# mLSTM trunk on one core: causal mask applied in the copy of the scores, three convolution steps given to the odd chunk

## The chip, the cores and the metric

The kernel runs on one core of a Trainium2 chip. The metric is the time of one execution in device microseconds; the number compared is the median of several runs. The engines are named as in the profile: PE is TensorE's matmul stream (PEld its weight loads), DVE is VectorE, ACT is ScalarE, POOL is GpSimd, and SP is the queue that issues most DMAs.

## The reference

One layer of a hybrid decoder on x (1, 4096, 1024): RMSNorm, one input projection, a pooling branch, an mLSTM branch with 4 heads of 256, an output projection, a residual sum and a final RMSNorm. What the change touches is the chunkwise mLSTM with chunks of 128 rows, inside which every row sees only itself and earlier rows:

```
xc = silu(causal_conv(mx, conv_w, conv_b))          # 4 taps
q, k = headwise(xc, w_q), headwise(xc, w_k)
v = headwise(mx, w_v)
...
mask = tril(ones(CHUNK, CHUNK))
d_log = where(mask, b[:, None] - b[None, :] + ig[None, :], -inf)
W = exp(d_log - m_t[..., None]) * einsum('bhcld,bhcsd->bhcls', q, k)
num = einsum('bhcls,bhcse->bhcle', W, v) + inter * (C_s q)
```

## The kernel before, in words

The program has three stages. The first (to about 800 us) normalises x and computes the pooling branch. The second (about 800 to 1740 us) projects the mLSTM input, convolves it and runs the 32 chunks. The third computes the output gates, the second gate path and the output projection with a Strassen-like scheme. Products in fp32 are made of three fp32r matmuls, high times high, high times low and low times high, so almost every operand exists as a pair of tiles. `split` (L103) makes the pair: ACT copies the high part (L104), and DVE, or POOL where that is asked for, subtracts it from the raw value to get the low part (L105).

In the second stage three generators advance side by side for chunk n.

- `front(n)` has 13 steps, each called an "f". Steps 1 to 3 make v (L774, the copies in L776). Steps 4 and 5 make the q side, `qg` (L784, copied by ACT in L786); step 5 needs channels 4 to 7 of the convolved input `xc`. Steps 6 and 7 make the scores (L795): ACT copies 128x256 of them out of PSUM into `sc` (L797), and DVE copies the gate sums into `part` (L798). Steps 8 and 9 turn `xc` (L804). Step 10 makes the forget gates `lf` (L808 to L815) and PE turns them (L818). Steps 11 and 12 run the two scans and spread the result over the partitions (L824 to L851). Step 13 makes the decay `dm`: ACT writes four exponentials (L863), POOL sets the entries of future rows to zero (L864), DVE multiplies by the scores (L866), and `split` (L867) makes the pair `wt`, which sits in the pool named `st`. Step 13 also makes the pairs `qi` (L872 on DVE, L874 on ACT, L875 on POOL).
- `back(n-1)` has 13 steps, each a "b". For each head it computes the numerator `num` (L901 from `wt` and v, L905 from `qi` and the state), then updates the state (L930 on PE, L931 on DVE). The third matmul of L901 needs the low part of `wt`, the last thing that step 13 makes.
- `project` of the next block of 256 rows has 17 steps, the first of them before the chunk pair and the others each a "p". The mLSTM input of two channel groups of 128 is projected in four steps (L111 to L113 into `acc`), then copied out by ACT (L750) and given its last tap (L755).

After every fourth "p" a `tail` waits in a list: six multiply-adds of DVE (L673) in two steps of three, and a third step, SiLU: three activations of ACT (L695 to L697), a product of DVE (L698) and a store (L699). A "c" in the order advances the first tail of the list by one step. There are four tails in a pair of chunks, called t0 to t3 here; the channels 6 and 7 of t3 are needed by step 5 of the next even chunk.

`ORDER` (L31) writes out the order of f, b, p and c, one string for even chunks and one for odd ones. Behind the string the kernel finishes step 13 of `front`, and after an odd chunk also the projection and the tails (L978 to L988). This order of the code is a priority: the framework's planner lays out each engine's queue by its own model of time and takes, whenever an engine comes free, the first in order among those that are ready by that model. Each engine then works its queue strictly in that planned order.

Of the kernel before, what the change touches and what calls it, by code (L numbers as in the profile page):

```python
# [8 lines left out]
F32 = mybir.dt.float32  # L9
# [3 lines left out]
ALU = mybir.AluOpType  # L13
# [4 lines left out]
P = 128  # L18
# [5 lines left out]
H = 4  # L24
# [3 lines left out]
TB = 256  # L28


ORDER = ("ffffbbffbpbffbpffppccbbbcbfpbfbbpppccc", "ffffbbbfpfffpbfbfppbccbbccfpbfpbppbbcc")  # L31
VA = P + 1
GW = P + 8

# [20 lines left out]
def tile_hybrid(  # L55
# [16 lines left out]
    nc = tc.nc  # L72
# [30 lines left out]
    def split(raw, hi, lo, eng=None):  # L103
        nc.scalar.copy(out=hi, in_=raw)  # L104
        (eng or nc.vector).tensor_tensor(out=lo, in0=raw, in1=hi.bitcast(F32), op=ALU.subtract)  # L105
# [274 lines left out]
    with tc.tile_pool(name="a_st", bufs=4) as stp, \  # L380
# [147 lines left out]
        for b in range(NB):  # L528
# [6 lines left out]
            for j in range(NJ):  # L535
                g = j // 2
                win = WINDOWS[g]
                ps = accp.tile([P, T], F32, name="acc")
# [12 lines left out]
                while step < win:  # L551
# [3 lines left out]
                                            op=ALU.add)  # L555
                    cur, lo_c, step = nxt, a, step * 2
                dlt = cur[:, HALO:]
                if b == 0:
# [4 lines left out]
                                               op0=ALU.mult, op1=ALU.subtract)  # L563
# [22 lines left out]
    with tc.tile_pool(name="b_mx", bufs=NJ) as mxp, \  # L586
# [35 lines left out]
        parts = [one.tile([64 + H, P], BF16, name=f"parts{i}") for i in range(2)]  # L622
        for t in parts:
            nc.vector.memset(t, 0.0)
        bif = one.tile([P, 8], F32, name="bif")
        nc.sync.dma_start(out=bif, in_=b_if.partition_broadcast(P))

# [12 lines left out]
        for j in range(NJ):  # L640
            bqT, bkT, bvT = ({j: t[j // 4][:, j % 4]} for t in bqkv)
            ps = mapp.tile([P, T], F32, name="map")
# [121 lines left out]
        def front(n, c, mx, xc):  # L764
# [6 lines left out]
            for w, (j0, nj) in enumerate(((0, 3), (3, 3), (6, 2))):  # L771
                ps = mapp.tile([P, 3, GW], F32, name="map")
# [8 lines left out]
            for q in range(2):  # L781
                ps = mapp.tile([P, 4, P], F32, name="map")
# [6 lines left out]
            sc = wk.tile([P, H, P], F32, name="sc", bufs=1)  # L789
            for q in range(2):  # L790
                ps = mapp.tile([P, 2, GW], F32, name="map")
                for hh in range(2):
                    for t in range(2):
                        j = 4 * q + 2 * hh + t
                        nc.tensor.matmul(ps[:, hh, :], lhsT=xc[j][:, l0:l0 + P], rhs=qg[:, j, :],  # L795
                                         start=t == 0, stop=t == 1)
                nc.scalar.copy(out=sc[:, 2 * q:2 * q + 2, :], in_=ps[:, :, 0:P])  # L797
                nc.vector.tensor_copy(out=part[:, :, 3 + 2 * q:5 + 2 * q], in_=ps[:, :, P:].rearrange("p i g -> p g i"))  # L798
                yield
            for q in range(2):  # L800
                if xs is not None:
                    ps = mapp.tile([P, 4, P], F32, name="map")
                    for i in range(4):
# [25 lines left out]
                                         op0=ALU.add, op1=ALU.add)  # L829
# [31 lines left out]
            dm = wk.tile([P, H, P], F32, name="dm", bufs=1)  # L861
            for h in range(H):
                nc.scalar.activation(out=dm[:, h, :], in_=dp[:, h, :], func=AF.Exp, bias=ibc[:, h:h + 1])  # L863
            nc.gpsimd.affine_select(out=dm, in_=dm, compare_op=ALU.is_ge, fill=0.0, base=0,  # L864
                                    pattern=[[0, H], [1, P]], channel_multiplier=-1)
            nc.vector.tensor_tensor(out=dm, in0=sc, in1=dm, op=ALU.mult)  # L866
            split(dm, wt[:, 0], wt[:, 1])  # L867
            qi = []
            for h in range(H if n else 0):
                q = wk.tile([P, 2, 2, P], F32R, name="qi", bufs=4)  # L870
                raw = wk.tile([P, 2, P], F32, name="qr", bufs=4)
                nc.vector.tensor_tensor(out=raw, in0=qg[:, 2 * h:2 * h + 2, 0:P],  # L872
                                        in1=inter[:, h:h + 1, :].broadcast_to([P, 2, P]), op=ALU.mult)
# [95 lines left out]
        for n in range(NB * NCH + 1):  # L969
            fr = Steps(front(n, n % 2, *xin), 13) if n < NB * NCH else None  # L970
            turn = {"f": fr, "b": bk, "p": proj}
            for what in ORDER[n % 2]:
                if what == "c":
                    step_tail()
                elif turn[what] is not None:
                    turn[what].step()
            if bk is not None:
                bk.finish()  # L978
            if fr is None:
                break  # L980
            if n + 1 == NB * NCH:
                proj.finish()
            bk = Steps(back(n // NCH, n % NCH, *fr.finish()), 5 if n + 1 == NB * NCH else 13)
            bk.step()
            if n % 2 and n + 2 < NB * NCH:
                xin = proj.finish()
                finish_tails()
                proj = start((n + 3) // 2) if (n + 3) // 2 < NS else Steps(next_operands(), 11)  # L988
# [311 lines left out]
```

## Time and profile before

| | us |
|---|---|
| median of 3 runs (3122.46 to 3127.13) | 3122.95 |
| the profiled execution | 3121.92 |
| its span, first to last instruction | 3120.2 |
| PE busy in the span | 2916.4 (93%) |
| DVE busy | 2103.1 (67%) |
| ACT busy | 1371.2 (44%) |
| POOL busy | 897.8 (29%) |

The profile lists each engine's busy time and idle time, and puts an idle stretch down to the instruction that ended it. The timeline gives start, duration, engine, line, output and input, and in brackets the idle time before and its releaser. In the answer for stretches of time the columns are the stretch, its length, busy time of each engine with its instructions, the granted TensorE clock as a share of the full one, the DMA share and GB/s. An instruction of DVE or ACT that follows another without waiting may start before the end of that other one as the profile writes it.

### The profile page before, as it was taken

The page shows a single profiled execution, that of the slowest core. Times are in us where ns is not written, and L with a number is a line of the kernel's source. Part 1 is how long each engine was busy: PE and PEld are TensorE (multiplying, and loading weights), DVE is VectorE, ACT ScalarE, POOL GpSimd, SP SyncE. Part 2 cuts the span into 40 slices and gives each one's busy share as a digit, 9 for nine tenths or more (in the row PEclk, how much of TensorE's full clock was granted, in tenths as well). Part 3 has the DMA queues.
Part 4 walks back from the last instruction along what each step waited for, and adds up shares of the span by engine and source line. Part 5 has one row for each costly group of instructions (what it writes and reads, how often), then busy time and mean ns, then how long its engine had stood idle before and what let it go on. Part 6 is the DMA issues. An engine that isn't in the chain of part 4 may idle for free. (4 is left out here: it accounts for less than half of the span.)

```text
span 3120.2 us, 44964 instructions
## 1 busy us (share of the span) xinstructions
PE 2916.4 (93%) x15912; PEld 2527.6 (81%) x15912; DVE 2103.1 (67%) x4107; ACT 1371.2 (44%) x2722; POOL 897.8 (29%) x955
## 2 busy tenths in 40 slices
PE   7999999998989999999998897998989899989998
PEld 6888888887889989989987676887777788867887
DVE  6555555564678878878878643667667866676666
ACT  4222222211667676677677311235556633343332
POOL 1122333333255455455453222001111133320000
PEclk9999999998999999999999899999999999999999
DMA  6344455545221121121123588686677888886664
GB/s 213 115 159 154 157 185 187 184 156 189 85 65 48 49 67 49 49 68 49 48 74 93 212 277 288 222 273 209 228 244 235 273 268 277 276 293 206 211 209 170
DMA packets 258001, 531.59 MB, mean 170 GB/s; under 512 B 28528, under 2 KB 72048, under 8 KB 257776
## 3 DMA queue, kind: packets, MB, share of 16 engines
q1 hardware_dynamic: 225952, 412.84, 38.4%
q10 hardware_dynamic: 31824, 115.88, 12.1%
q8 instruction: 125, 2.05, 0.3%
q14 instruction: 100, 0.82, 0.1%
HBM read 331.49 MB, written 197.13 MB: 169 GB/s over the span
## 5 line engine op out<-in xcount | busy, mean ns | idle before, releaser
L111 PE MATMUL ps<-w,sr 128*128 128x512 f32 x1320 | 524.1, 397 | 28.0 <-ACT sr L104 19.6
L113 PE MATMUL ps<-w,sr 128*128 128x512 f32 x1320 | 520.4, 395 | 15.1 <-DVE sr L105 15.0
L112 PE MATMUL ps<-w,sr 128*128 128x512 f32 x1320 | 521.3, 395 | 0.0
L105 DVE TENSOR_TENSOR sr<-sr 128x1024 fp32r<-128x1024 f32 x221 | 285.6, 1295 | 299.8 <-ACT sr L104 298.8
L104 ACT CAST sr<-sr 128x1024 fp32r<-128x1024 f32 x221 | 231.1, 1048 | 529.2 <-PE ps L112 274.3
L111 PE MATMUL acc<-u,w 128*128 128x512 f32 x1024 | 398.8, 390 | 1.5 <-ACT u L104 1.5
L112 PE MATMUL acc<-u,w 128*128 128x512 f32 x1024 | 398.8, 389 | 0.0
L113 PE MATMUL acc<-u,w 128*128 128x512 f32 x1024 | 398.6, 389 | 0.0
L111 PEld LDWEIGHTS ps<-w,sr 128*128 128x128 f32 x1320 | 252.5, 191 | 84.4 <-ACT sr L104 21.7
L113 PEld LDWEIGHTS ps<-w,sr 128*128 128x128 f32 x1320 | 251.5, 191 | 71.6 <-DVE sr L105 19.1
L111 PE MATMUL acc<-xu,w 128*128 128x256 f32 x992 | 295.7, 298 | 0.0
L112 PEld LDWEIGHTS ps<-w,sr 128*128 128x128 f32 x1320 | 252.2, 191 | 52.8 <-issue 0.7
L113 PE MATMUL acc<-xu,w 128*128 128x256 f32 x992 | 287.2, 290 | 0.0
L112 PE MATMUL acc<-xu,w 128*128 128x256 f32 x992 | 284.4, 287 | 0.0
L661 POOL TENSOR_TENSOR cs<-c,cs 128x516 fp32r<-128x516 f32 x124 | 177.7, 1433 | 219.9 <-ACT cs L660 193.5
L673 DVE SCALAR_TENSOR_TENSOR xc<-mx,col,xc 128x256 f32<-128x256 f32 x384 | 221.6, 633 | 13.1 <-ACT xc L755 11.5
L111 PEld LDWEIGHTS acc<-u,w 128*128 128x128 f32 x1024 | 192.1, 188 | 42.3 <-ACT u L104 2.2
L113 PEld LDWEIGHTS acc<-u,w 128*128 128x128 f32 x1024 | 192.2, 188 | 40.2
L112 PEld LDWEIGHTS acc<-u,w 128*128 128x128 f32 x1024 | 192.2, 188 | 40.1
L111 PEld LDWEIGHTS acc<-xu,w 128*128 128x128 f32 x992 | 194.0, 196 | 1.2
L112 PEld LDWEIGHTS acc<-xu,w 128*128 128x128 f32 x992 | 194.1, 196 | 0.1
L113 PEld LDWEIGHTS acc<-xu,w 128*128 128x128 f32 x992 | 193.8, 195 | 0.0
(229 smaller groups left out, 5968.1 us busy)
## 6 DMA issues: line engine op xcount, KB each, us to landing
sr<-us_d ACTq DMA_DIRECT2D x112, 512.0 KB, 5.2
us_d<-st SPq DMA_DIRECT2D x64, 512.0 KB, 2.7
sr<-ym_d ACTq DMA_DIRECT2D x56, 512.0 KB, 4.4
sr<-yp_d ACTq DMA_DIRECT2D x53, 512.0 KB, 5.5
st<-in_x_t_dram SPq DMA_DIRECT2D x32, 512.0 KB, 6.0
yp_d<-sg SPq DMA_DIRECT2D x64, 256.0 KB, 2.7
st<-us_d SPq DMA_DIRECT2D x32, 512.0 KB, 5.8
xu<-us_d SPq DMA_DIRECT2D x64, 256.0 KB, 3.6
```

The costliest lines, as they stand in the source:

```text
L104: nc.scalar.copy(out=hi, in_=raw)
L105: (eng or nc.vector).tensor_tensor(out=lo, in0=raw, in1=hi.bitcast(F32), op=ALU.subtract)
L111: nc.tensor.matmul(ps, lhsT=a[0], rhs=b[0], start=start and k == 0, stop=False, skip_group_check=skip)
L112: nc.tensor.matmul(ps, lhsT=a[0], rhs=b[1], start=False, stop=False, skip_group_check=skip)
L113: nc.tensor.matmul(ps, lhsT=a[1], rhs=b[0], start=False, stop=stop and k == n - 1, skip_group_check=skip)
L661: nc.gpsimd.tensor_tensor(out=t[:, 1], in0=cst[h], in1=t[:, 0].bitcast(F32), op=ALU.subtract)
L673: nc.vector.scalar_tensor_tensor(out=a[:, t], in0=m[:, t, i:i + TB], scalar=conv_w[:, jj * 4 + i:jj * 4 + i + 1], in1=a[:, t], op0=ALU.mul ...
```

## The change

The zeroing on POOL goes. Instead a 128x128 tile `causal` of ones and zeros is made once, and the copy of the scores out of PSUM becomes a DVE product with that tile, in steps 6 and 7 of `front`, in place of ACT's copy. As the decay of future rows is now not zeroed and may overflow, the product of decay and scores first limits the decay to 3e38. In the order, the "ccc" at the end of the even chunk (all of tail t1) moves into the odd chunk, behind its first "p".

```
-ORDER = ("ffffbbffbpbffbpffppccbbbcbfpbfbbpppccc", "ffffbbbfpfffpbfbfppbccbbccfpbfpbppbbcc")
+ORDER = ("ffffbbffbpbffbpffppccbbbcbfpbfbbppp", "ffffbbbfpcccfffpbfbfppbccbbccfpbfpbppbbcc")
...
+        causal = one.tile([P, P], F32, name="causal")
+        nc.vector.memset(causal, 1.0)
+        nc.gpsimd.affine_select(out=causal, in_=causal, compare_op=ALU.is_ge, fill=0.0, base=0,
+                                pattern=[[1, P]], channel_multiplier=-1)
...
-                nc.scalar.copy(out=sc[:, 2 * q:2 * q + 2, :], in_=ps[:, :, 0:P])
+                nc.vector.tensor_tensor(out=sc[:, 2 * q:2 * q + 2, :], in0=ps[:, :, 0:P],
+                                        in1=causal.unsqueeze(1).broadcast_to([P, 2, P]), op=ALU.mult)
...
-            nc.gpsimd.affine_select(out=dm, in_=dm, compare_op=ALU.is_ge, fill=0.0, base=0,
-                                    pattern=[[0, H], [1, P]], channel_multiplier=-1)
-            nc.vector.tensor_tensor(out=dm, in0=sc, in1=dm, op=ALU.mult)
+            nc.vector.scalar_tensor_tensor(out=dm, in0=dm, scalar=3e38, in1=sc, op0=ALU.min, op1=ALU.mult)
```

## The prediction

> **What bounds the kernel now.** I read the page first, then stretches of the stage that changes, then PE's waits there, then the timelines of all engines around the longest wait.
>
> ```profile
> PE 2916.4 (93%) x15912; PEld 2527.6 (81%) x15912; DVE 2103.1 (67%) x4107; ACT 1371.2 (44%) x2722; POOL 897.8 (29%) x955
> ```
>
> ```profile
> 817.00:1686.00 869.00, 809.78 (x6497) 787.70 (x6497) 703.15 (x1952) 611.59 (x1483) 409.87 (x523) 0.96 0.18 58
> 1009.77:1036.16 26.39, 26.39 (x222) 25.81 (x221) 21.29 (x65) 19.06 (x48) 11.41 (x16) 1.00 0.12 39
> 1036.16:1067.91 31.75, 27.93 (x223) 27.05 (x222) 26.21 (x69) 22.15 (x55) 17.08 (x22) 0.95 0.22 69
> 1042.81:1046.22 3.41, 3.41 (x18) 3.41 (x19) 3.41 (x13) 3.21 (x8) 1.13 (x1) 0.57 0.02 8
> 878.89:882.30 3.41, 3.41 (x29) 3.38 (x30) 2.68 (x9) 0.24 (x1) 0.00 (x0) 1.00 0.00 0
> ```
>
> PE bounds the kernel, and the mLSTM stage too: in 869 us it is busy for 809.78, DVE for 703.15. The second and third rows are one odd and one even chunk. They hold the same PE work (222 and 223 matmuls), but the odd chunk is filled to the end and the even one takes 5.36 us more. Where that goes, PE's waits (800 to 1700 us) and its timeline say:
>
> ```profile
> PE mm L901 <- DVE st L105: 38.7, 14, 2.8
> PE map L818 <- DVE lf L815: 8.5, 15, 1.8
> ```
>
> ```profile
> 1039.76 0.28 PE L112 MATMUL acc<-xu,w 128*128 128x256 f32 x1
> ...
> 1042.81 0.58 PE L901 MATMUL mm<-va,st 128*128 128x258 f32 x1 [2.77 <-DVE st L105]
> ...
> 1046.81 0.61 PE L784 MATMUL map<-xc,bqk 128*128 128x128 f32 x4
> ```
>
> Fourteen times, once in a pair of chunks, the third matmul of head 0's numerator waits 2.77 us for the low part of `wt`. The 3.41 us behind that wait have a granted clock of 0.57, and only 18 matmuls pass. PE's busy time in the even chunk is 27.93 us against 26.39 in the odd one, about 1.4 us more after the one extra matmul: that is the price of the clock. Wait and clock together are 4.2 of the 5.36 us.
>
> Why is the low part late? DVE, ACT and POOL at the end of odd chunk 7:
>
> ```profile
> 1035.91 1.22 DVE L866 TENSOR_TENSOR dm<-sc,dm 128x512 f32<-128x512 f32 x1 [1.71 <-POOL dm L864]
> 1037.05 0.86 DVE L931 SCALAR_TENSOR_TENSOR c<-c,decay,mm 128x258 f32<-128x258 f32 x2
> 1037.83 4.32 DVE L673 SCALAR_TENSOR_TENSOR xc<-mx,col,xc 128x256 f32<-128x256 f32 x6
> 1042.08 0.68 DVE L105 TENSOR_TENSOR st<-dm,st 128x512 fp32r<-128x512 f32 x1
> ...
> 1044.54 0.69 DVE L698 TENSOR_TENSOR xc<-xc,sgm 128x512 f32<-128x512 f32 x1
> ```
>
> ```profile
> 1034.63 0.39 ACT L863 ACTIVATE dm<-map,ibc 128x128 f32<-128x128 f32 x1
> ...
> 1036.10 0.62 ACT L750 COPY mx<-acc 128x512 f32<-128x512 f32 x1
> 1036.58 1.06 ACT L755 ACTIVATE xc<-acc,col 128x256 f32<-128x256 f32 x2
> 1037.48 0.66 ACT L104 CAST st<-dm 128x512 fp32r<-128x512 f32 x1
> ...
> 1042.19 0.63 ACT L695 ACTIVATE sgm<-xc 128x512 f32<-128x512 f32 x1 [2.35 <-DVE xc L673]
> ```
>
> ```profile
> 1033.95 1.34 POOL L661 TENSOR_TENSOR cs<-c,cs 128x516 fp32r<-128x516 f32 x1 [3.03 <-ACT cs L660]
> 1035.24 0.64 POOL L864 TENSOR_SCALAR_AFFINE_SELECT dm<-dm 128x512 f32<-128x512 f32 x1
> 1035.84 3.44 POOL L875 TENSOR_TENSOR qi<-qr,qi 128x256 fp32r<-128x256 f32 x4
> ```
>
> The exponentials end at 1035.02. The select stands behind L661 on POOL, so the product starts at 1035.91. The high part is copied at 1037.48, behind L750 and L755. By then the first three multiply-adds of t3 are ready on DVE; they come first in the code, so all six go first, 4.32 us, and the subtraction that PE needs starts at 1042.08. At the end of the next, even chunk it is the other way round:
>
> ```profile
> 1067.42 1.22 DVE L866 TENSOR_TENSOR dm<-sc,dm 128x512 f32<-128x512 f32 x1 [0.53 <-POOL dm L864]
> ...
> 1070.31 0.68 DVE L105 TENSOR_TENSOR st<-dm,st 128x512 fp32r<-128x512 f32 x1
> 1070.91 2.45 DVE L673 SCALAR_TENSOR_TENSOR xc<-mx,col,xc 128x256 f32<-128x256 f32 x6
> ```
>
> ```profile
> 1068.68 0.62 ACT L104 CAST st<-dm 128x512 fp32r<-128x512 f32 x1 [0.53 <-DVE dm L866]
> 1069.20 0.58 ACT L750 COPY mx<-acc 128x512 f32<-128x512 f32 x1
> ```
>
> Here the high part is copied before L750, the subtraction goes before the six of t1, and PE does not wait. So the order on DVE hangs on whether the product is through before the projection comes out.
>
> **The change part by part.** Durations of the operations concerned:
>
> ```profile
> L105 DVE TENSOR_TENSOR va<-map,va 128x256 fp32r<-128x256 f32 x27 | 11.1, 410 | 0.0
> ```
>
> ```profile
> L797 ACT COPY sc<-map x64: 363/373/383, 819.3 to 1722.4; 128x256 f32<-128x256 f32 x64
> ```
>
> ```profile
> L866 DVE TENSOR_TENSOR dm<-sc,dm x32: 678/1219/1229, 835.7 to 1735.9; 128x512 f32<-128x512 f32 x32
> ```
>
> ```profile
> L562 DVE SCALAR_TENSOR_TENSOR sum<-sum,z x64: 673/692/2766, 44.2 to 750.2; 128x512 f32<-128x512 f32 x64
> ```
>
> ```profile
> DVE part L798 <- ACT sc L797: 24.0, 30, 3.6
> ```
>
> *Masked copy.* ACT loses 64 copies of 0.373 us, and DVE gains 64 products of 128x256 out of PSUM. The nearest row is the same shape from PSUM, 0.410: 0.82 us a chunk. Where DVE now idles for ACT's copy (24.0 us over 30 waits, 0.8 each) the product takes the place of the wait, so I put the net on DVE at 0 to 0.82 us a chunk, and take 0.2. Behind it on DVE stand L798 and the gates, and PE's L818 waits for those. ACT has idle time, so its 0.75 us a chunk buys nothing by itself.
>
> *Product with limit.* The trace has no minimum-and-multiply; a fused operation of 128x512 on two SBUF inputs has 0.692 as median (L562), the plain product 0.678 to 1.229. I take 1.22, the row it is nearest to, because POOL's L875 still runs beside it; bounds 0.68 (a gain of 0.54 on the way to `wt`) and 1.23. The GPSIMD Engine Reference of the Trainium skill, section Key points, says that POOL shares its SBUF interfaces with DVE and collides with DVE instructions that read two SBUF inputs; by that the limit keeps the long price and the mask, with one PSUM input, does not have it.
>
> *Select removed.* The product can start with the last exponential, 1035.02, ends at 36.24 and not 37.13: 0.89 us earlier. POOL's L875 moves up by up to 0.64 us; nothing waits for that. The one select that makes `causal`, and its memset, run before the first chunk: by L864's row 0.64 us, at most that once.
>
> *What this does at the boundary.* If the order of the queues stays, L931 follows by about 37.1, when the first L755 is through too (half of its 1.06), and the six start 0.7 us earlier than at 37.83. The wait falls from 2.77 to about 2.1: gain 0.7 us. If the order flips as at the even chunk's end, ACT copies the high part at 36.24 to 36.9, the subtraction runs to 37.6, and PE does not wait for it. But L750 and L755 move back by about 0.7 us, and the next thing late is t3 itself. From the end of the six to the end of L698 it takes 3.1 us now (42.15 to 45.23), and the second half of step 5 (L784 at 1046.81) needs that. With st and L931 first the six run from 38.4: to 42.7 at the long price, xc by 45.8, 1.0 us before 46.81; to 40.85 at the short price of 2.45, xc by 43.95, 2.9 us before. PE has then too little else to do until then, so a wait of 2 to 3 us remains in another place, and with it the slow clock. So 0.7, or 1.0 to 2.9; a flip being likelier than not, I take 1.6 us a pair.
>
> *The steps of t1.* Six L673, three activations, L698 and the store L699 move from before step 13 of the even chunk to behind the first "p" of the odd one. At the even end they already ran behind the subtraction, with no PE wait. The odd chunk has 26.39 − 21.29 = 5.1 us of idle DVE that covers them; the price without that cover is in the rival below. On SP the store moves past loads of the next projection only in the code's order; DMA share is 0.12 there. I put this part at 0.
>
> Sum: 14 pairs times 1.6 = 22 us, less the masks' 0.2 in the even chunks only, 3 us, plus the 0.64: about −19 to −22. Against the profiled execution's 3121.92 (span 3120.2, 1.7 around it; the median of the runs is 1.03 higher) that is 3101.
>
> **The rivals.** *The wait goes altogether, and the slow clock with it.* For: the odd chunk shows the same PE work in 26.39 us. Against: t3's chain. Gain 14 × (2.77 + 1.4) = 58 us: 3064. The clock decides a third of it.
>
> ```profile
> 878.89 0.27 PE L818 MATMUL map<-ident,lf 128*4 128x128 f32 x1 [1.77 <-DVE lf L815]
> ```
>
> This 1.77 us wait is followed by a clock of 1.00 (the stretch from 878.89 above), the 2.77 us one by 0.57, so it is enough to bring the wait below 1.8. TensorE: Matmul & The Clock Gate of the Trainium skill, under HAM oscillation, wants gaps above about 3.4 us before the clock falls; by that these waits would cost no clock and the gain would be 39 us, 3083. The 0.57 speaks against it.
>
> *Slower: the gates of the odd chunk.* Two rows of odd chunk 7:
>
> ```profile
> 1020.72 0.16 DVE L815 SCALAR_TENSOR_TENSOR lf<-g,ef 128x4 f32<-128x4 f32 x1 [0.75 <-ACT ef L813]
> ```
>
> ```profile
> 1022.47 0.27 PE L818 MATMUL map<-ident,lf 128*4 128x128 f32 x1
> ```
>
> `lf` is ready 1.59 us before PE turns it. If t1's six run beside POOL, at 4.32 and not 2.45, and the masks' 0.82 come on top, `lf` is 2.69 us later, and PE waits 1.1 us in each odd chunk. With the boundary unchanged that is 15 × 1.1 = 17 us: 3139. It decides once DVE is more than 1.59 us late at L815.
>
> *Nothing.* The planner keeps the order, L673 starts no earlier because L755 sets it, and the masks eat the rest: within 6 us.
>
> **How the numbers follow.** A shortened or moved wait with 0.7 to 2.9 us a pair (3112 to 3081), 0.50; the wait and the clock gone, 0.19; nothing, 0.15; slower, 0.16. The likeliest gives 3101. The range from 3063 to 3126 leaves out most of the slower case and a little of the best one. A measurement of this kernel can tell about 0.2%, 6 us: faster 0.69, same 0.15, slower 0.16.
>
> **What would show it.** No POOL row on `dm`; L866's line follows ACT's exponential with no idle above 1 us. At the odd end the subtraction into `st` stands before the six L673 (flip) or within 1 us of them as now. PE's wait of L901 for `st` falls from 38.7 us; in its place a wait of L784 for `xc`, or of L818 for `lf`. Even chunk near 30 us, odd chunk at 26.4. Wrong would be: even chunks at 31.7 as before, or odd chunks above 27.5, or a loss outside 800 to 1740 us.

## The result and the profile after

The kernel after takes 3106.91 us (median, 3102.35 to 3110.42) against 3122.7 for the kernel before beside it: a ratio of 0.9944 with an interval of 0.9931 to 0.9958, faster by 0.6%. Two of the twelve executions of one kernel further down, the one with later multiply-adds, took 4778 and 10052 us at mean granted clocks of 0.56 and 0.28, and its ratio leaves them out. The profiled execution took 3106.23 us, its span is 3104.5. The engine row of its page:

```profile
PE 2903.6 (94%) x15912; PEld 2520.3 (81%) x15912; DVE 2116.8 (68%) x4172; ACT 1352.9 (44%) x2658; POOL 883.5 (28%) x924
```

PE has the same 15912 matmuls and is busy 12.8 us less, because more of them ran at the full clock. The stretches (the whole stage, odd chunk 7, the even chunk behind it, and 3.41 us behind the wait between the two):

```profile
817.00:1686.00 869.00, 808.97 (x6583) 788.55 (x6581) 740.66 (x2057) 607.26 (x1451) 402.11 (x497) 0.98 0.19 61
1004.50:1030.29 25.79, 25.79 (x220) 25.40 (x219) 21.59 (x67) 18.32 (x44) 9.97 (x14) 1.00 0.10 34
1030.29:1061.90 31.61, 28.09 (x221) 27.26 (x220) 26.91 (x71) 21.46 (x53) 17.24 (x21) 0.95 0.22 68
1037.31:1040.72 3.41, 3.41 (x20) 3.41 (x21) 3.41 (x10) 3.41 (x8) 1.60 (x2) 0.68 0.00 0
```

In the same 869 us 6583 matmuls are recorded instead of 6497, at 0.98 of the clock and not 0.96. Yet this even chunk is hardly shorter than before (31.61 against 31.75): it still holds a wait and, behind it, a fallen clock. PE's waits (800 to 1700 us) say where the wait now stands, and the timelines of DVE, ACT, POOL and PE at the end of chunk 7 say why:

```profile
PE mm L936 <- DVE ws L894: 27.1, 13, 2.1
PE map L825 <- DVE lf L822: 13.5, 16, 2.2
...
PE mm L907 <- DVE st L105: 2.0, 1, 2.0
```

```profile
1029.87 0.79 DVE L872 SCALAR_TENSOR_TENSOR dm<-dm,sc 128x512 f32<-128x512 f32 x1 [0.84 <-ACT dm L870]
1030.93 0.88 DVE L937 SCALAR_TENSOR_TENSOR c<-c,decay,mm 128x258 f32<-128x258 f32 x2 [0.27 <-PE mm L936]
1031.73 0.77 DVE L105 TENSOR_TENSOR st<-dm,st 128x512 fp32r<-128x512 f32 x1
1032.43 4.44 DVE L678 SCALAR_TENSOR_TENSOR xc<-mx,col,xc 128x256 f32<-128x256 f32 x6
1036.79 0.87 DVE L894 SCALAR_TENSOR_TENSOR ws<-st,wcol,ws 128x256 fp32r<-128x256 f32 x2
...
1039.60 1.33 DVE L703 TENSOR_TENSOR xc<-xc,sgm 128x512 f32<-128x512 f32 x1
```

```profile
1030.70 0.62 ACT L104 CAST st<-dm 128x512 fp32r<-128x512 f32 x1
1031.22 0.58 ACT L755 COPY mx<-acc 128x512 f32<-128x512 f32 x1
1031.70 1.02 ACT L760 ACTIVATE xc<-acc,col 128x256 f32<-128x256 f32 x2
```

```profile
1030.21 2.88 POOL L881 TENSOR_TENSOR qi<-qr,qi 128x256 fp32r<-128x256 f32 x3
...
1033.39 0.98 POOL L881 TENSOR_TENSOR qi<-qr,qi 128x256 fp32r<-128x256 f32 x1
1034.41 1.38 POOL L742 TENSOR_TENSOR xu<-xu 128x512 fp32r<-128x512 f32 x1
```

```profile
1033.67 0.61 PE L907 MATMUL mm<-va,st 128*128 128x258 f32 x3
...
1034.84 0.40 PE L936 MATMUL mm<-va,ws 128*128 128x258 f32 x2
1037.31 0.75 PE L936 MATMUL mm<-va,ws 128*128 128x258 f32 x4 [2.08 <-DVE ws L894]
```

(Line numbers are five to seven higher than before: L673 is now L678, L750 is L755, L866 is L872, L888 is L894, L930 is L936.) The order on DVE has flipped: the product follows the last exponential, ACT copies the high part of `wt` before the projection's output (L755), and the subtraction into `st` (1031.73) stands ahead of the six multiply-adds of t3. The numerator waits for `st` once (2.0 us) and no longer fourteen times. But the six still stand in DVE's queue as one block of 4.44 us, and the next product that PE needs stands behind them: the low part of `ws`, the weighted k rows that the state update (L936) uses. PE waits 2.08 us there instead of 2.77, thirteen times.

### The profile page after: what moved, and what is told of

Same layout as the page of the kernel before. It is cut to its first block, busy times and chain, and to the rows that moved or that the text cites. A ratio compares the mean times of both kernels' runs of the same rounds, so it can differ in the third digit from the quotient of the medians.

```text
span 3104.5 us, 45002 instructions
## 1 busy us (share of the span) xinstructions
PE 2903.6 (94%) x15912; PEld 2520.3 (81%) x15912; DVE 2116.8 (68%) x4172; ACT 1352.9 (44%) x2658; POOL 883.5 (28%) x924
## 5 line engine op out<-in xcount | busy, mean ns | idle before, releaser
L113 PEld LDWEIGHTS ps<-w,sr 128*128 128x128 f32 x1320 | 251.3, 190 | 74.5 <-DVE sr L105 22.2
L678 DVE SCALAR_TENSOR_TENSOR xc<-mx,col,xc 128x256 f32<-128x256 f32 x384 | 226.2, 642 | 15.2 <-ACT xc L760 11.5
```

The costliest lines, as they stand in the source:

```text
L113: nc.tensor.matmul(ps, lhsT=a[1], rhs=b[0], start=False, stop=stop and k == n - 1, skip_group_check=skip)
L678: nc.vector.scalar_tensor_tensor(out=a[:, t], in0=m[:, t, i:i + TB], scalar=conv_w[:, jj * 4 + i:jj * 4 + i + 1], in1=a[:, t], op0=ALU.mul ...
```

## The experiments

The theory that came out of the two traces: the change acts through the order of DVE's queue alone, and what PE waits for now is held by the block of six multiply-adds. The rivals are that the moved steps or the masked copies carry part of the time, and that the wait belongs to the chain of one product (t3, `ws`, the numerator) and not to DVE. Each run was timed beside the kernel before, on the same chip; ratios are to that. Diffs are against the kernel after.

**The two parts apart.** First the mask with the old order of steps:

```
-ORDER = ("ffffbbffbpbffbpffppccbbbcbfpbfbbppp", "ffffbbbfpcccfffpbfbfppbccbbccfpbfpbppbbcc")
+ORDER = ("ffffbbffbpbffbpffppccbbbcbfpbfbbpppccc", "ffffbbbfpfffpbfbfppbccbbccfpbfpbppbbcc")
```

> The masked copy and the product with limit, but the order of the steps as before. Theory A (the select behind the decay kept the subtraction into wt behind six multiply-adds; taking it away alone turns that order round): nearly the whole gain, 3104 to 3111 us, and PE's wait of L907 for st at head 0 gone, a wait of about 2 us for ws in its place. Theory B (the three moved steps relieve DVE and bring the gain): 3119 to 3125 us.

3104.97 us, ratio 0.9947 (0.9935 to 0.9959). Its waits:

```profile
PE mm L936 <- DVE ws L894: 27.1, 13, 2.1
PE map L825 <- DVE lf L822: 11.7, 15, 1.0
```

The wait that matters is that of the kernel after to the last digit, and so is the time, as theory A had it. The whole gain comes with the mask; the steps of t1, moved into the odd chunk, add nothing to it.

Then the new order of steps alone, with the select on GpSimd and ACT's copy of the scores as in the kernel before:

```
-                nc.vector.tensor_tensor(out=sc[:, 2 * q:2 * q + 2, :], in0=ps[:, :, 0:P],
-                                        in1=causal.unsqueeze(1).broadcast_to([P, 2, P]), op=ALU.mult)
+                nc.scalar.copy(out=sc[:, 2 * q:2 * q + 2, :], in_=ps[:, :, 0:P])
...
-            nc.vector.scalar_tensor_tensor(out=dm, in0=dm, scalar=3e38, in1=sc, op0=ALU.min, op1=ALU.mult)
+            nc.gpsimd.affine_select(out=dm, in_=dm, compare_op=ALU.is_ge, fill=0.0, base=0,
+                                    pattern=[[0, H], [1, P]], channel_multiplier=-1)
+            nc.vector.tensor_tensor(out=dm, in0=sc, in1=dm, op=ALU.mult)
```

> The select on POOL and ACT's copy of the scores as before, only the three steps of t1 moved into the odd chunk. Theory A: 3119 to 3126 us, the wait of L901 for st unchanged at 2.8 us in 14 pairs, because the multiply-adds that stand before it are those of t3 and not of t1. Theory B: 3104 to 3112 us.

3115.96 us, ratio 0.9986 (0.9977 to 0.9995), between the two ranges that were expected. The wait of the numerator for `st` is as before (40.4 us over 15 waits, the longest 2.8). The 0.14% is at the edge of what can be told here; no wait in the trace explains it.

**What the mask costs where it went.** Scores copied by ACT again, with no select anywhere. This kernel leaves the zeroing of future rows out:

```
-                nc.vector.tensor_tensor(out=sc[:, 2 * q:2 * q + 2, :], in0=ps[:, :, 0:P],
-                                        in1=causal.unsqueeze(1).broadcast_to([P, 2, P]), op=ALU.mult)
+                nc.scalar.copy(out=sc[:, 2 * q:2 * q + 2, :], in_=ps[:, :, 0:P])
```

> As the changed kernel, but the scores are copied by ACT and future rows are not masked at all, so the 64 masked copies of 0.41 us on DVE are left out. Theory A with hidden masks: 3102 to 3109 us, no more than 5 us from the changed kernel. Rival (the masked copies cost what the wait of L825 for lf in even chunks rose by, 0.4 us in 14 pairs, and more): 3094 to 3100 us.

3109.33 us, ratio 0.9966 (0.9954 to 0.9979): not faster than the kernel after. In the kernel after the masked copies are the first row below; the second is the longest wait beside that for `ws` in the run without them.

```profile
L803 DVE TENSOR_TENSOR sc<-map,causal x64: 407/424/426, 820.2 to 1705.2; 128x256 f32<-128x256 f32 x64
```

```profile
PE map L824 <- DVE lf L821: 20.7, 17, 2.1
```

64 products of 0.424 us are 27 us of DVE time, and trading them for ACT's copies gains nothing: the masked copies cost no more than what they replaced. PE's wait for the gates (`lf`) is longer without them, not shorter.

**The select alone, put back.** One edit, POOL's select in front of the product (the masked copies stay, so the mask is applied twice):

```
+            nc.gpsimd.affine_select(out=dm, in_=dm, compare_op=ALU.is_ge, fill=0.0, base=0,
+                                    pattern=[[0, H], [1, P]], channel_multiplier=-1)
             nc.vector.scalar_tensor_tensor(out=dm, in0=dm, scalar=3e38, in1=sc, op0=ALU.min, op1=ALU.mult)
```

> As the changed kernel with POOL's select put back in front of the product (the masked copy stays, so the mask is applied twice). Theory A (the select alone decided the order on DVE): the six multiply-adds stand before the subtraction into st again, PE's wait of L907 for st is back at 2.8 us in 14 pairs, 3118 to 3130 us. Rival (the gain came from ACT's copies taken away or from the masked copies): 3104 to 3112 us.

3118.14 us, ratio 0.999 (0.9978 to 1.0002): the gain is gone, the six stand ahead of the subtraction again (4.32 us at most boundaries), and the old wait is back.

```profile
PE mm L909 <- DVE st L105: 38.4, 14, 3.0
```

So 0.64 us of POOL between the exponentials and the product decided which of two blocks the planner put first on DVE, and that is the whole effect of the change, as far as 0.2% can be told.

**What holds the new wait?** Three attempts to move something out from in front of `ws`. First, later multiply-adds: the last "cc" of the odd order, t3's, dropped, so that they are laid out behind the code of the boundary:

```
-ORDER = ("ffffbbffbpbffbpffppccbbbcbfpbfbbppp", "ffffbbbfpcccfffpbfbfppbccbbccfpbfpbppbbcc")
+ORDER = ("ffffbbffbpbffbpffppccbbbcbfpbfbbppp", "ffffbbbfpcccfffpbfbfppbccbbccfpbfpbppbb")
```

> As the changed kernel, but the last two steps of the odd order (the multiply-adds of t3) are left to the end of the chunk, behind step 13, so that the two subtractions into ws stand among the six and not behind them. Theory C (the 2.08 us wait for ws is a matter of queue order): it goes, PE next waits for the second half of step 5 or for nothing, 3075 to 3098 us. Rival D (t3's own chain up to xc is as late as ws): PE waits for xc in its place, 3100 to 3110 us. If the slow clock behind the wait goes too, 1.4 us a pair more.

3131.53 us, ratio 1.0034 (1.0022 to 1.0046): slower, and both theories missed.

```profile
PE map L800 <- DVE part L782: 34.8, 15, 2.4
PE mm L936 <- DVE ws L894: 11.7, 13, 0.9
```

The planner left three of the six ahead of `ws` and put three among the copies of v. The wait for `ws` fell to 0.9 us, and a longer one came up one product further on: the PSUM banks in which v was made (`map`) come free only when DVE has subtracted and summed them. At the boundary behind chunk 7 the first of these sums ends at 1043.57 us, and L800 starts at 1043.63.

Second, fewer of them. This kernel leaves three of the four taps of channel group 7 out, three of the six multiply-adds of t3:

```
-                for i in range(3):
+                for i in range(0 if jj == NJ - 1 else 3):
```

> As the changed kernel, but the last channel group of every block keeps only its last tap: three of the six multiply-adds of t3 are left out (2.2 us of DVE at the long price at the boundary, as many 128x256 products less in all as there are blocks times three). Theory E (DVE is what the boundary waits for, whatever stands in front of what): PE's 2.08 us wait for ws goes, no slow clock behind it, 14 pairs times 2.1 to 3.6 us: 3056 to 3077 us. Rival F (another chain, ACT's or the path up to xc, is as late): a wait of 1 us or more stays in another place, 3085 to 3103 us.

3085.55 us, ratio 0.9882 (0.9865 to 0.99), at the fast edge of rival F's range. Half of the block gone brings some 20 us, but a wait stays in another place, as F had it:

```profile
PE map L789 <- DVE r L916: 25.9, 14, 2.0
```

By the timeline it is again the `map` banks, freed late because DVE is late, and not ACT or `xc` as F had it: the first sum over them (L782) ends at 1032.62 us, and PE goes on at 1032.76. The releaser named (L916) is only the instruction that DVE ended last before that.

Third, other work for PE: the numerators computed one head ahead of the updates.

```
-            for h in range(H):
...
+            order = "0 1 00 01 2 10 11 3 20 21 30 31" if not last else "0 1 2 3"
+            for k, what in enumerate(order.split()):
...
+                if len(what) == 1:
+                    num_of(int(what))
+                else:
+                    update(int(what[0]), int(what[1]))
```

> As the changed kernel, but each head's numerator is computed one head ahead of the state updates (0, 1, update 0, 2, update 1, 3, ...), so that PE has 1.08 us more work in front of the first update at the boundary. Theory: the wait for ws falls to about 1.0 us, too short for the slow clock, but xc of t3 still sets step 5; 3080 to 3100 us. Rival D (all PE gains before step 5 it waits there): 3100 to 3110 us.

3110.95 us, ratio 0.9966 (0.9953 to 0.9978): no gain over the kernel after, just above rival D's range. PE passes `ws` and waits for the same banks, not for `xc` as D had it.

```profile
PE map L800 <- DVE part L782: 26.7, 14, 2.0
```

These three say the same: at the boundary DVE itself is behind, and PE waits for whichever of its products it comes to. What helps is less DVE time there.

**Why the six take 4.44 us.** In the kernel before, six multiply-adds of the same shape (t1's) took 2.45 us at the end of even chunks. The difference beside them is that POOL is not subtracting there. This kernel leaves the low part of q out (POOL writes zeros in its place); every queue keeps its order:

```
-                nc.gpsimd.tensor_tensor(out=q[:, 1], in0=raw, in1=q[:, 0].bitcast(F32), op=ALU.subtract)
+                nc.gpsimd.memset(q[:, 1].bitcast(F32), 0.0)
```

> As the changed kernel, but POOL writes zeros into the low part of qi instead of subtracting, so q keeps only its high part; the order of DVE's queue is unchanged. Theory G (DVE's multiply-adds take 0.72 us and not 0.40 because POOL's two-input subtractions run beside them): the six of t3 fall from 4.44 to 2.5 to 3.0 us, PE's wait for ws from 2.08 to 0.2 to 0.7, the slow clock is gone: 3060 to 3080 us. Rival (their length has another cause, such as the dependence of each on the one before): the six stay above 4 us, 3100 to 3108 us.

3063.6 us, ratio 0.9815 (0.9796 to 0.9835). DVE and PE's waits in that run:

```profile
1083.56 2.50 DVE L678 SCALAR_TENSOR_TENSOR xc<-mx,col,xc 128x256 f32<-128x256 f32 x6
1085.99 1.89 DVE L894 SCALAR_TENSOR_TENSOR ws<-st,wcol,ws 128x256 fp32r<-128x256 f32 x2
```

```profile
PE mm L936 <- DVE ws L894: 14.3, 14, 1.1
```

The six take 2.50 us instead of 4.44, and the wait halves, though 0.2 to 0.7 us were expected. With that the clock does not fall once between 860 and 1650 us (below).

**The same without leaving work out.** The kernel after, complete, in which POOL's subtractions for heads 1 to 3 at the end of an odd chunk are queued behind the last subtraction for the next block's rows that the code lists (`u_low`); in POOL's queue that is the second of the four at the boundary. The queues of the other engines are unchanged, instruction by instruction:

```
+                u_low.append(nc.gpsimd.tensor_tensor(out=lo, in0=raw, in1=hi.bitcast(F32), op=ALU.subtract))
...
+                if n % 2 and h and (n + 3) // 2 < NS:
+                    q_late.append((q, raw))
+                else:
+                    low_q(q, raw)
...
                 proj = start((n + 3) // 2) if (n + 3) // 2 < NS else Steps(next_operands(), 11)
+                if q_late:
+                    with tc.issue_after(u_low[-1].ins):
+                        for q in q_late:
+                            low_q(*q)
+                    q_late.clear()
```

> The kernel after, complete, with one order changed: at the end of an odd chunk GpSimd's subtractions of the low parts of q for heads 1 to 3 are queued behind the second subtraction of the low part of the next block's rows (xu), so that they no longer run beside the six multiply-adds of t3. The queues of the other four engines are as in the kernel after. Theory G (GpSimd's two-input subtractions beside the six lengthen them, and nothing else holds the boundary): the six take about 3.0 us instead of 4.44, the wait for the low part of ws falls from 2.1 us to 0.5 to 1.0 us a pair, and with waits this short the half clock windows nearly go, as without the low part of q: 13 x 1.3 us of wait and 8 to 17 us of clock, 3072 to 3088 us. Rival H (the subtractions only collide with other work: the numerator of head 1 waits for its q, or the VectorE work behind the boundary becomes as much longer, by some 3 x 0.3 us a pair and more): the wait for ws falls but a wait for qi or for the scores' row of work takes its place, 3098 to 3115 us.

3068.25 us, ratio 0.9838 (0.9821 to 0.9854): the fastest complete kernel of this study, and faster than was expected; by the ratios it lies another 1.1% of the time of before below the kernel after, some 33 us. DVE, POOL and PE at one boundary, then PE's waits and the stretch from 860 to 1630 us:

```profile
1079.60 0.68 DVE L105 TENSOR_TENSOR st<-dm,st 128x512 fp32r<-128x512 f32 x1
1080.20 2.50 DVE L678 SCALAR_TENSOR_TENSOR xc<-mx,col,xc 128x256 f32<-128x256 f32 x6
1082.62 1.89 DVE L903 SCALAR_TENSOR_TENSOR ws<-st,wcol,ws 128x256 fp32r<-128x256 f32 x2
```

```profile
1082.29 1.55 POOL L748 TENSOR_TENSOR xu<-xu 128x512 fp32r<-128x512 f32 x1 [1.96 <-ACT xu L747]
1085.36 1.28 POOL L748 TENSOR_TENSOR xu<-xu 128x512 fp32r<-128x512 f32 x1 [1.52 <-ACT xu L747]
1086.61 2.75 POOL L735 TENSOR_TENSOR qi<-qr,qi 128x256 fp32r<-128x256 f32 x3
```

```profile
1084.18 0.74 PE L945 MATMUL mm<-va,ws 128*128 128x258 f32 x4 [1.06 <-DVE ws L903]
```

```profile
PE mm L945 <- DVE ws L903: 14.3, 14, 1.1
```

```profile
860.00:1630.00 770.00, 731.47 (x6093) 713.60 (x6092) 661.66 (x1886) 552.97 (x1326) 379.50 (x467) 1.00 0.19 60
```

POOL idles for 1.96 us behind ACT while the six run, and they take 2.50. The collision has moved to the next pair: the two `ws` products take 1.89 beside L748 where they took 0.87 without it. A wait of 1.06 is left, and the mean clock of the stretch is 1.00.

Beside it, the same with head 1 left in its old place:

> As the run beside it, but only the subtractions for heads 2 and 3 are queued later; that for head 1 stays beside the six multiply-adds. Theory G: the six are lengthened by one subtraction more (about 0.3 to 0.5 us) than in the run beside it, the wait for ws stands at 0.9 to 1.4 us a pair, and the time lies 4 to 12 us above that run's: 3078 to 3098 us. Rival H (head 1's q comes too late when it is moved): this one is the faster of the two, by the wait for qi that it saves.

3073.37 us, ratio 0.9859 (0.9836 to 0.9882). The interval overlaps the run before: head 1's place is not told apart, and the expectation that the six grow by 0.3 to 0.5 us was wrong (2.45 us in this run).

**What is the change worth once the six are short?** The last kernel has the late subtractions and the select in front of the product again, so the six stand ahead of `st`, as in the kernel before:

> The kernel with q's low parts for heads 1 to 3 queued later (the first of the two runs before), and the select on GpSimd back in front of the product, as in the kernel before: VectorE's queue has the six multiply-adds ahead of the subtraction into st again. What is the change itself worth once the six are short? Theory G (the length of the six sets the boundary, their place little): product, two updates, six and subtraction take 0.7 to 1.2 + 0.9 + 2.5 + 0.7 us instead of 1.22 + 0.86 + 4.32 + 0.68, so that the wait for st falls from 2.8 us to 0.7 to 1.2 us a pair, too short for the half clock windows: 3066 to 3082 us, within some 10 us of the kernel without the select. Rival I (the select and the order hold st back whatever the six take): 2.0 us a pair or more stay, with the windows: 3092 to 3106 us.

3103.7 us, ratio 0.9946 (0.9931 to 0.996): theory G missed, and the time and the wait are those of rival I. The late subtractions without the flip bring 0.5%, the change alone 0.6%, both together 1.6%.

```profile
1028.35 1.22 DVE L880 SCALAR_TENSOR_TENSOR dm<-dm,sc 128x512 f32<-128x512 f32 x1 [1.72 <-POOL dm L878]
1029.49 0.86 DVE L948 SCALAR_TENSOR_TENSOR c<-c,decay,mm 128x258 f32<-128x258 f32 x2
1030.28 3.46 DVE L678 SCALAR_TENSOR_TENSOR xc<-mx,col,xc 128x256 f32<-128x256 f32 x6
1033.66 0.68 DVE L105 TENSOR_TENSOR st<-dm,st 128x512 fp32r<-128x512 f32 x1
```

```profile
PE mm L918 <- DVE st L105: 26.0, 14, 2.1
```

With the select the product waits 1.72 us and still takes 1.22 beside POOL, and the six, now later, run into L748 and take 3.46. The wait is 1.9 to 2.1 us, as long as the kernel after's, and the time is the kernel after's too. Each edit takes PE's wait from 2.8 to about 2; only both take it to 1.1, and only there the clock stays up.

## Why the prediction was right, and where it failed

**What bounds.** Right. PE bounds the stage, and each pair of chunks loses a wait, and most pairs a fallen clock behind it, at one place. The cause was named rightly too: the run with the select put back shows that the select decides the order of DVE's queue.

**The flip.** Right as written: the high part before the projection's output (L750 there, L755 now), the subtraction before the six, the numerator without a wait (13 of 14 times).

**"The next thing late is t3 itself".** This step failed. `xc` was not late: waits of PE for L703 are 0.2 us in all between 800 and 1700 us. I followed the six forward to what they make and overlooked what stands behind them in the same queue. On DVE the row behind the six was `ws`, and PE reaches the state update 1.2 us after the numerator (1033.67 to 1034.84), well before step 5 needs `xc`. The forecast wait in another place did come, with nearly the forecast length (2.08 us; 2 to 3 were written) and with the slow clock behind it, so the sum came out near for a reason of the wrong name; that part was luck.

**The sum.** 1.6 us a pair was forecast. The product's row after, beside L866's in the prediction:

```profile
L872 DVE SCALAR_TENSOR_TENSOR dm<-dm,sc x32: 679/796/1249, 835.0 to 1717.3; 128x512 f32<-128x512 f32 x32
```

From the first product to the last it is 882.3 us, and was 900.2: 17.9 us over 15 boundaries, 1.2 a pair, inside the bounds of 0.7 to 2.9. The span fell by 15.7 us where 19 to 22 were forecast. The last product starts 18.6 us earlier than before, so 2.9 us were given back behind it, and no run here shows by what.

**The terms that were off.** The product with the limit took 0.79 at this boundary and not 1.22 (bounds 0.68 to 1.23): it starts 0.34 us ahead of POOL's subtractions for q (1029.87 and 1030.21), where before it started just behind the first of them (1035.91 and 1035.84). At the end of even chunks it still starts behind one and takes 1.23. The multiply-adds took the long price, 4.44. The masked copies cost no more than the copies they replaced (the run without a mask), where I had put 3 us. The wait of PE for `lf` grew from 8.5 to 13.5 us between 800 and 1700 us, 5.0 us that I had only in the slower rival; the run without the masked copies has 20.7 us there, so the masks do not make it. What does stays open.

**The clock.** I priced a fallen clock at 1.4 us a pair, from one pair. From the first product to the last PE was busy for 825.2 us before and 814.8 after, and idle for 75.0 and 67.5. So of the 17.9 us, 10.4 are matmuls that ran at a higher clock and 7.5 are shorter waits; PE's longer wait for `lf` is already in the latter. By the starts of the product at the odd ends, thirteen pairs can be compared. Before, ten took 58.1 to 58.4 us, and three with a fallen clock of double length 59.7 to 60.5. After, nine with a fallen clock behind the boundary took 57.1 to 57.9, and the four in which it stayed up 55.4 to 56.7. So the price was about right, but a shorter wait with the clock still falling is worth only 0.2 to 0.5 us in most pairs, and 12.3 of the 18.1 us gained over the thirteen come from those four. Which pairs they are depends on where the wait lies on the clock's grid (last section). The prediction did not know of that, and that there were four is luck.

**The rivals.** "The wait goes altogether" gave 3064, and that is nearly where the kernel with the later subtractions lies (3068), though with a wait of 1.06 left. Its condition, a wait below 1.8 us, was of the right kind, as the clock stays up behind waits of 1.1 us. But the wait of 1.77 us from which it was taken lay across two steps of the clock (1.37 and 0.40 us in them), so it did not show what a wait of that length costs. The TensorE: Matmul & The Clock Gate page of the Trainium skill, section HAM oscillation, lets the clock fall at gaps above about 3.4 us; the runs do not agree, with ten falls in the stretch where PE waited 2.08 us a pair. The slower rival and "nothing" did not come.

## What to carry to other kernels

When an edit takes an instruction out from behind a block in an engine's queue, read the queue on behind the block before pricing the gain: the wait goes to the first product there that the bounding engine reaches, not to the end of the block's own chain. When the same instructions have two durations in one profile, look at what the neighbouring engine does beside the long ones; here ending that was worth 1.1% on top of the new order, and 0.5% without it. And price a wait with what follows it: two edits that each took it from 2.8 to 2 us gave 0.5 to 0.6%, both together 1.6%, and only then was it too short for the clock to fall.

## What the runs showed of the hardware

**VectorE beside GpSimd.** A multiply-add of 128x256 with two SBUF inputs takes 0.41 us when POOL does not subtract beside it (2.45 for six), and 0.74 when POOL subtracts one SBUF tile from another (4.44 for six). Which of the two starts first matters: in the kernel after, the product of 128x512 takes 0.79 us where it starts 0.34 us ahead of a subtraction (1029.87), and 1.23 where it starts 0.06 us behind one (1061.65). Where POOL only writes zeros (the kernel without q's low part) it takes 0.68, though it starts while they are being written (1054.88, POOL from 1054.62 to 1055.18). The masked copies, with one of their two inputs in PSUM, take 0.41 to 0.43 us, beside a subtraction or not. The SBUF — State Buffer page of the Trainium skill, section Who interferes with whom, says that a VectorE instruction with two SBUF inputs collides with a GpSimd instruction that reads SBUF and not with one that only writes it; these runs agree.

**The clock and the length of the wait.** Missing clock between 860 and 1650 us, as the sum over the clock record of the share that is missing, in steps of half a microsecond:

| kernel | wait at the boundary, us | missing clock, us (stretches) |
|---|---|---|
| before | 2.8 | 29.0 (14) |
| new order alone | 2.8 | 23.9 (12) |
| select put back | 3.0 | 18.8 (10) |
| later multiply-adds | 0.9 and 2.4 | 32.4 (13) |
| mask alone | 2.1 | 22.2 (13) |
| after | 2.1 | 17.1 (10) |
| select, late subtractions | 2.1 | 17.1 (10) |
| half of t3 | 2.0 | 15.4 (9) |
| numerators ahead | 2.0 | 10.2 (6) |
| no mask | 2.4 | 10.2 (6) |
| late subtractions, heads 2 and 3 | 1.1 | 3.4 (2) |
| late subtractions | 1.1 | 1.7 (1) |
| no low part of q | 1.1 | 0 (0) |

(The wait is the longest one of its row.) At boundaries with a wait of 1.1 us the clock never falls: the stretches in the last rows stand behind other waits, of 2.2 us and about 4 us, near the end of the stage.

With waits of 2 us and more it falls in six to fourteen of the pairs, and the traces show why not in all. Every fallen stretch lasts one or more steps of 3.41 us, and in each trace all of them start a whole number of such steps apart: the clock is granted on a fixed grid. What counts is how long PE idles within one step. Two waits of 2.1 us in the kernel after, each time the step that holds most of the wait and the step behind it:

```profile
1035.14:1038.55 3.41, 1.33 (x11) 1.24 (x11) 3.41 (x8) 1.87 (x5) 0.65 (x1) 1.00 0.00 0
1038.55:1041.96 3.41, 3.41 (x18) 3.41 (x18) 3.41 (x13) 2.93 (x6) 2.84 (x2) 0.50 0.03 9
1495.94:1499.35 3.41, 1.56 (x13) 1.56 (x14) 3.41 (x10) 1.98 (x4) 0.32 (x1) 1.00 0.01 2
1499.35:1502.76 3.41, 3.26 (x28) 3.06 (x28) 3.41 (x11) 2.96 (x7) 3.17 (x3) 1.00 0.12 39
```

The first wait (1035.24 to 1037.31) lies within one step, in which PE idles for 2.08 us, and the next step has a clock of 0.50. The second (1495.70 to 1497.79) lies across two steps; 1.85 us of idle time fall into the later one, and the clock stays up. Counted over the thirteen kernels of the table from 860 to 1650 us, PE idled for 1.9 us or more in 101 of the 105 steps at full clock that a fallen one followed (1.7 to 1.9 in the other four), and in none of the 2771 steps at full clock that no fallen one followed. So a wait of 2 us costs clock when it fits into one step and not when it is split, and rows with the same wait differ by where their waits lie on the grid. These are counts over the traces; no run here moved a wait on the grid on purpose.
